# A planner learns that weight buffers take turns, and rounds the next weights after a block's first step

## The chip, the core and the metric

The kernel runs on one core of a Trainium2 chip. The metric is device time in microseconds: the median of three runs of the kernel before is 920.47 us (920.26 to 920.74). Engines are named as the profile names them: PE (TensorE, with PEld for its weight loads), DVE (VectorE), ACT (ScalarE), POOL (GpSimd), SP (SyncE).

## The reference

Two layers of a streaming encoder, with the same weights for a new stream of 512 frames (the prompt) and for 64 frames of a running one (the sample, with a cache of 1024 frames). Cut to what matters:

```python
def layer(x, ...):
    h = rms_norm(x, norm_g)
    u_p, z_p, q, k, v, qi, ki, wi, z_a, g_p, g_a = split(h @ w_in)
    pooled = causal means of u_p over 2, 4, 8, 16 frames, minus u_p, mixed by w_pool_mix
    br_pool = (pooled * silu(z_p)) @ w_pool_out
    q, k, qi, ki = rope(...)                       # 8 heads of 64; indexer 8 heads of 32
    score = sum_h wi * relu(qi . ki)               # the indexer; chunk-causal mask
    o = softmax(q . k over the top 128 (prompt) or 256 (sample) by score) @ v
    br_attn = (o * silu(z_a)) @ w_attn_out
    x = x + (sigmoid(g_p) * br_pool + sigmoid(g_a) * br_attn) @ w_o
    return x, k, v, ki, pool_state
y = rms_norm(x after two layers, final_norm_g)
```

All of it is float32, and so are the outputs.

## The kernel before

**Tiling.** The model's 1024 columns lie on the 128 partitions in 8 parts; the 576 frames (512 + 64) are the free dimension. All weights are cut into pieces of 128 x 1024, 57 in each layer. A piece comes from memory into a buffer `raw` (a load that SP issues). It is then split (`split_to`, L342): ACT rounds it to the matmul's format (the high part, `CAST whl<-raw`), ACT writes the raw weights' negative beside it (`ACTIVATE whl<-raw`), and POOL issues a DMA that adds the raw weights to it, which leaves the low part. Three buffers `whl` take turns. Activations are kept as a high part `h` and a low part `lo` as well.

**Blocks.** A block (`block`, L461) multiplies one piece by all frames: 8 steps (`step`, L440) of 6 matmuls of 128x288, which are high times high, high times low and low times high for each half of the frames. So a block is 48 matmuls, in the profile `mm<-quart,whl`. Into them other work is woven: the pooling mixer, the indexer's scores and the selection, the attention of the prompt by heads and query tiles (512, 384, 256 and 128 wide), then that of the sample.

**What sets the order.** The program is unrolled ahead of time. `Plan` (L62) runs its own clock for each engine while the program is written: `run` (L143) sets each instruction's start by when its operands and its engine are ready, by costs given for each kind of instruction. The woven work is written as generators. Each yields a condition (`need`, L208), and after each step of a block `pump` (L230) takes those whose condition holds by these clocks. `slot` (L176) is how most buffers tell the plan when a new tile of a ring can be written: not before the last use of the tile that it replaces. The `whl` buffers were not told of: the plan takes a new one as writable at once. On the chip each engine works its own instructions off in the order written, and a wait at the head of an engine's queue holds all that is behind it.

**The places in question.** At the start of a block its weights are taken and the piece three ahead is split (`block`, L461 to L463): ACT's two instructions and POOL's DMA are written ahead of the block's first matmul. At the start of layer 0, `Entry.first` (L498) rounds the eight parts of x on ACT as they arrive, and after the first of them `ki_split` rounds the indexer's key weights. Every instruction is written through one helper, so all rows of the profile bear line 262 (263 in the changed kernel).

Names: `sm` are score and transpose results, `mm` those of blocks (both in PSUM); `prob` and `quart` also hold probabilities, `tmp` anything of 128x576; `Ct` and `St` are the rope tables times the norm's factors, made by POOL; `qz`, `qzl` are the prompt's queries, `qzs` the sample's; `ident` marks a transpose; `stat` holds row sums.

Of the kernel before, what the change touches and what calls it, by code (L numbers as in the profile page):

```python
# [11 lines left out]
F32R = mybir.dt.float32r  # L12
# [3 lines left out]
P = 128  # L16
# [30 lines left out]
UNITS = 3  # L47
FIRST_H = ()
LAG = (1, 2)
DMA_US = 3.0  # L50
WARM = 11
NORM_A = 0
# [12 lines left out]
class Plan:  # L65
# [77 lines left out]
    def run(self, eng, op, args, kw):  # L143
# [18 lines left out]
        if eng == "dma" or op == "dma_start":  # L162
            n = 1
            for k in outs[0].shape[1:]:
                n *= k
            late = DMA_US + 4 * outs[0].shape[0] * n / 180e3
        for x in outs:
# [100 lines left out]
def encoder_step(ctx: ExitStack, tc: tile.TileContext, a: dict):  # L268
    nc = tc.nc
    plan = Plan()  # L270
# [5 lines left out]
    rot = ctx.enter_context(tc.tile_pool(name="rot", bufs=1))  # L276
# [7 lines left out]
    def tmp(n=T, dtype=F32):  # L284
        return rot.tile([P, 608], dtype, name="tmp", tag="tmp", bufs=NTMP)[:, :n]
# [16 lines left out]
    def ps_mm():  # L302
        return plan.slot("mm", 2, psum.tile([P, 2, 512], F32, name="mm", tag="mm", bufs=2), False)

    def ps_s(hold=False):
        return plan.slot("sm", 4, psum.tile([P, 512], F32, name="sm", tag="sm", bufs=4), hold)
# [22 lines left out]
    for l in range(DEPTH):  # L329
        pieces += [(l, j) for j in range(a["n_pieces"])]  # L330
    raw_of, split_of = {}, {}
    state = {"load": 0, "split": 0, "next": 0}

    def load_to(n):
        while state["load"] < min(n, len(pieces)):
            i = state["load"]
            l, j = pieces[i]
            raw_of[i] = raws()
            dma.dma_start(raw_of[i], a["w"][l, j])
            state["load"] += 1  # L340

    def split_to(n):  # L342
        while state["split"] < min(n, len(pieces)):
            i = state["split"]
            load_to(i + 1)
            x = raw_of.pop(i)
            w = rot.tile([P, 2, 1024], F32R, name="whl", tag="whl", bufs=3)
            act.copy(w[:, 0], x)

            act.activation(w[:, 1], x, AF.Copy, scale=-1.0)  # L350
            pool.dma_start(w[:, 1].bitcast(F32), x, accum_op=OP.add)
            plan.let(x)
            split_of[i] = w
            state["split"] += 1

    def split_first(i=0):

        load_to(i + 1)
        x = raw_of.pop(i)
        w = rot.tile([P, 2, 1024], F32R, name="whl", tag="whl", bufs=3)  # L360
        for c, eng in ((slice(0, 512), dve), (slice(512, 1024), pool)):
            act.copy(w[:, 0, c], x[:, c])
            eng.tensor_tensor(w[:, 1, c], x[:, c], w[:, 0, c].bitcast(F32), op=OP.subtract)
        plan.let(x)
        split_of[i] = w
        state["split"] = i + 1

    def weights():
        i = state["next"]
        state["next"] += 1  # L370
        split_to(i + 1)
        load_to(i + 4)
        w = split_of.pop(i)
        return w, i
# [60 lines left out]
    ps = ps_s()  # L435
# [3 lines left out]
    def step(ps, w, xh, xl, k, nk, off=0, parts=((0, 0, HT), (1, HT, T)), low=(False, True)):  # L439

        c = slice(off + k * P, off + (k + 1) * P)
        wh, wl = w[:, 0, c], w[:, 1, c]
        for s, t0, t1 in parts:
            cols = slice((k % 2) * T + t0, (k % 2) * T + t1)
            h, lo = xh[k // 2][:, cols], xl[k // 2][:, cols]
            o = ps[:, s, :t1 - t0]
            if False in low:  # L450
                pe.matmul(o, lhsT=wh, rhs=h, start=k == 0, stop=False)
                pe.matmul(o, lhsT=wh, rhs=lo, start=False, stop=False)
            if True in low:
                pe.matmul(o, lhsT=wl, rhs=h, start=False, stop=k == nk - 1)

    def product(ps, w, xh, xl, nk, off=0):
        for k in range(nk):
            step(ps, w, xh, xl, k, nk, off)
            plan.pump()

    def block(xh, xl, nk=8):  # L461
        w, i = weights()
        split_to(i + 3)  # L463
        ps = ps_mm()
        product(ps, w, xh, xl, nk)
        return ps

    class Entry:
# [29 lines left out]
        def first(self, k, x, ki_split):  # L498

            c = slice((k % 2) * T, (k % 2 + 1) * T)  # L500
            g = gains[:, self.l, k:k + 1]
            h = self.h[k // 2][:, c]
            if k in FIRST_H:
                dve.tensor_scalar(h, x, g, None, op0=OP.mult)
            else:
                act.activation(h, x, AF.Copy, scale=g)
            if k == 0:
                ki_split()
            dve.scalar_tensor_tensor(self.lo[k // 2][:, c], x, g, h.bitcast(F32), op0=OP.mult, op1=OP.subtract)
            self.rest.append(x)  # L510
            if k == 7:
                for i, x in enumerate(self.rest):
                    sq = tmp() if i else self.acc
                    act.activation(sq, x, AF.Square)
                    if i:
                        dve.tensor_tensor(self.acc, sq, self.acc, op=OP.add)
# [27 lines left out]
    def prepare_ki(l):  # L544
        rk = prob()
        rki = rk[:, :320].rearrange("p (k c) -> p k c", k=8)
        dma.dma_start(rk[:, :320], a["w_ki"][l])

        def ki_split():
            act.copy(kiw[:, :, 0:40], rki)  # L550
            (pool if l else dve).tensor_tensor(kiw[:, :, 64:104], rki, kiw[:, :, 0:40].bitcast(F32), op=OP.subtract)

        return ki_split

    def layer(l, x, arrive):
# [12 lines left out]
        if l:  # L568
            split_to(n + 3)
# [8 lines left out]
        ps_k, ps_q0 = [ps_s(True) for _ in range(2)], ps_mm()  # L578
        lag = (0, 0) if l else LAG
        for k in range(8 + lag[1]):  # L580
            if k == 7:
                plan.finish(*x.coming)
            if 3 <= k + 2 < 8:
                arrive(k + 2)
            if k < 8:
                c = (k % 2) * T
                for s in range(2):
                    cols = slice(c + s * HT, c + (s + 1) * HT)
                    pe.matmul(ps_k[s][:, :HT], lhsT=kiw[:, k], rhs=xh[k // 2][:, cols], start=k == 0, stop=False)
                for s in range(2):  # L590
                    cols = slice(c + s * HT, c + (s + 1) * HT)
                    pe.matmul(ps_k[s][:, :HT], lhsT=kiw[:, k], rhs=xl[k // 2][:, cols], start=False, stop=k == 7)
            if lag[0] <= k < 8 + lag[0]:
                step(ps_q0, w, xh, xl, k - lag[0], 8, low=(False,))
            if k >= lag[1]:
                step(ps_q0, w, xh, xl, k - lag[1], 8, low=(True,))
                plan.pump()
            if l == 0 and k == 4:
                split_first(1)
            if l == 0 and k == 6:  # L600
                split_to(3)
# [244 lines left out]

        def u_job(g):
            ps = block(xh, xl)
            ux = tmp(608)
            pool.memset(ux[:, 0:PST], 0.0)  # L850
# [39 lines left out]

        def z_job(g):
            ps = block(xh, xl)
            zt = tmp()
            dve.tensor_tensor(halves(zt), ps[:, :, :HT], halves(Rt), op=OP.mult)
# [35 lines left out]
        def sigmoid_gate():  # L930
            ps = block(xh, xl)
            zt = tmp()
            dve.tensor_tensor(halves(zt), ps[:, :, :HT], halves(Rt), op=OP.mult)

            def go():
                yield lambda: need("act", zt)
                act.activation(zt, zt, AF.Sigmoid)

            start(go(), 2)
            return zt  # L940
# [6 lines left out]
        def po_job(m2):  # L947
            if m2 == 0:
                plan.finish(*mixes)
            w, n = weights()  # L950
            split_to(n + 3)
            for i in range(2):
                ps = ps_mm()
                product(ps, w, ah, al, 4, off=512 * i)
                pb = sgs.pop(2 * m2 + i)
                dve.tensor_tensor(halves(pb), ps[:, :, :HT], halves(pb), op=OP.mult)

                def go(pb=pb, m=2 * m2 + i):
                    yield lambda: need("dma", pb)
                    dma.dma_start(mp_d[l][m], pb)  # L960

                start(go(), 2)
            if m2 == 3:
                let(*ah, *al)
# [492 lines left out]
    ki_split = prepare_ki(0)  # L1457
# [7 lines left out]
    def arrive(k):  # L1465
        x.first(k, xt[k // 2][:, (k % 2) * T:(k % 2 + 1) * T], ki_split)
        if k == 7:
            plan.let(*xt)
        if k == 1:
            split_first()  # L1470
# [110 lines left out]
```

## Time and profile before

| | us |
|---|---|
| median of 3 runs | 920.47 |
| profiled execution | 921.1 |
| its span, first to last instruction | 919.3 |
| PE busy | 894.8 (97%) |
| DVE busy | 668.3 (73%) |
| ACT busy | 593.2 (65%) |
| POOL busy | 202.1 (22%) |

The mean granted clock of PE is 0.995. By the chain of work that ended last, PE holds 68% of the span, DVE 14%, ACT 13%. A row of the timeline below gives the start, the time until the last of its instructions ended, the engine, the operation and its tiles, the count, and in brackets how long the engine had been idle before it and what released it. Times are microseconds from the start of the span. The rows stand in order of time, each engine works its rows in order, so what stands late in one engine's rows can be held by a row before it.

### The profile page before, as it was taken

The numbers are of one execution on the slowest core, as the hardware profiler recorded it, in microseconds if no ns is written. First come the engines' busy times: TensorE is split into PE (matmuls) and PEld (weight loads), VectorE is DVE, ScalarE is ACT, GpSimd is POOL, SyncE is SP. The second block draws the span as 40 slices with busy tenths as digits, with TensorE's granted clock in tenths as the row PEclk, the third lists the DMA queues.
The fourth block names the chain that finished last, engine by engine and source line by source line (L and its number), as shares of the span: only waits on it lengthen the run. The fifth ranks groups of instructions, "written<-read, shape, count | busy, mean of one in ns | idle before, by whom it ended". The sixth has DMA issues, their size and how long they took to land.

```text
span 919.3 us, 17403 instructions
## 1 busy us (share of the span) xinstructions
PE 894.8 (97%) x6613; PEld 881.4 (96%) x6613; DVE 668.3 (73%) x1554; ACT 593.2 (65%) x1056; POOL 202.1 (22%) x217
## 2 busy tenths in 40 slices
PE   8999999999999999999999999999999999999996
PEld 7999999999999999999999999999999999999995
DVE  6996899799896677362359779988989875755314
ACT  7556534588898975564537564446889988556642
POOL 3111211134432300112211121113443222011121
PEclk9999999999999999999999999999999999999998
DMA  7756587766555675779976667786655548648862
GB/s 266 187 140 164 134 214 189 173 161 160 125 145 147 179 199 150 186 202 240 263 191 175 154 151 163 191 203 180 165 139 133 157 124 221 189 135 222 236 146 104
DMA packets 54500, 160.97 MB, mean 175 GB/s; under 512 B 6736, under 2 KB 9040, under 8 KB 54416
## 3 DMA queue, kind: packets, MB, share of 16 engines
q0 software_dynamic: 16416, 59.78, 34.8%
q1 hardware_dynamic: 38000, 100.08, 32.2%
q8 instruction: 52, 0.85, 0.4%
q14 instruction: 32, 0.26, 0.1%
HBM read 85.37 MB, written 14.69 MB: 109 GB/s over the span
## 4 chain that ended last, share of the span: by engine, by line
PE 68%; DVE 14%; ACT 13%; issue 3%; DMA 1%; POOL 1%; SPq 0%; DVEq 0%; ACTq 0%; POOLq 0%
PE mm L262 57%; PE sm L262 11%; DVE tmp L262 6%; DVE quart L262 6%; ACT prob L262 4%; ACT whl L262 3%; ACT quart L262 2%; ACT qz L262 1%; ACT L262 1%; DVE big L262 1%; ACT tmp L262 1%; POOL tmp L262 1%; DMA raw<-in_w_dram 1%; DMA prob<-in_c_v_dram 1%; DVE prob L262 0%
## 5 line engine op out<-in xcount | busy, mean ns | idle before, releaser
L262 PE MATMUL mm<-quart,whl 128*128 128x288 f32 (+1 forms) x5568 | 780.4, 296 | 1.6 <-ACT quart L262 1.2
L262 PEld LDWEIGHTS mm<-quart,whl 128*128 128x128 f32 x5568 | 754.2, 188 | 4.3 <-ACT quart L262 2.0
L262 POOL DMA_DIRECT2D whl<-raw x114 | 99.3, 871 | 648.9 <-ACT whl L262 433.1
L262 ACT CAST whl<-raw 128x1024 fp32r<-128x1024 f32 (+1 forms) x118 | 121.8, 1034 | 133.2 <-PE mm L262 88.7
L262 ACT ACTIVATE whl<-raw 128x1024 fp32r<-128x1024 f32 x114 | 120.4, 1056 | 0.0
L262 ACT ACTIVATE prob<-prob,stat 128x128 f32<-128x128 f32 (+3 forms) x128 | 67.5, 554 | 6.8 <-DVE stat L262 6.4
L262 DVE SCALAR_TENSOR_TENSOR quart<-prob,wcol,quart 128x256 f32<-128x256 f32 (+4 forms) x60 | 42.1, 704 | 26.4 <-ACT prob L262 25.1
L262 ACT ACTIVATE prob<-sm 128x256 f32<-128x256 f32 (+4 forms) x72 | 33.5, 481 | 38.4 <-PE sm L262 38.4
L262 DVE MATCH_REPLACE8 quart<-stat,quart 128x256 f32<-128x256 f32 (+2 forms) x96 | 51.1, 539 | 0.0
L262 DVE MAX8 stat<-quart 128x8 f32<-128x256 f32 (+2 forms) x96 | 47.3, 541 | 0.0
L262 DVE MAX8 quart<-quart 128x8 f32<-128x544 f32 x64 | 46.3, 723 | 1.2
L262 DVE MATCH_REPLACE8 quart<-quart 128x544 f32<-128x544 f32 x64 | 45.4, 709 | 0.0
L262 DVE TENSOR_TENSOR tmp<-tmp 128x576 f32<-128x576 f32 (+7 forms) x62 | 44.3, 720 | 1.3
L262 DVE TENSOR_TENSOR quart<-quart 128x576 fp32r<-128x576 f32 (+6 forms) x30 | 26.4, 881 | 21.5 <-ACT quart L262 21.0
L262 DVE TENSOR_TENSOR big<-sm,big 128x512 fp32r<-128x512 f32 (+1 forms) x64 | 28.9, 483 | 16.3 <-ACT big L262 16.1
L262 ACT CAST quart<-tmp 64x512 fp32r<-64x512 f32 (+4 forms) x44 | 24.1, 566 | 22.0 <-POOL tmp L262 11.7
L262 ACT COPY prob<-sm 64x512 f32<-64x512 f32 (+1 forms) x24 | 12.3, 514 | 39.0 <-PE sm L262 38.6
L262 PE MATMUL sm<-quart,big 128*128 128x128 f32 (+3 forms) x176 | 32.2, 291 | 1.4 <-DVE tmp L262 1.4
L262 ACT CAST big<-sm 128x512 fp32r<-128x512 f32 (+2 forms) x72 | 28.0, 434 | 8.4 <-PE sm L262 8.0
L262 DVE SCALAR_TENSOR_TENSOR quart<-tmp,gains,quart 128x576 fp32r<-128x576 f32 x8 | 6.5, 818 | 31.6 <-ACT quart L262 31.6
L262 DVE CUSTOM_DVE_ANT_0 prob<-sm,quart 128x512 f32<-128x512 f32 (+2 forms) x48 | 25.8, 550 | 4.8 <-PE sm L262 4.8
L262 DVE TENSOR_TENSOR quart<-mm,tmp 128x576 f32<-128x576 f32 (+2 forms) x10 | 6.4, 638 | 29.3 <-PE mm L262 29.3
(157 smaller groups left out, 1025.5 us busy)
## 6 DMA issues: line engine op xcount, KB each, us to landing
raw<-in_w_dram SPq DMA_DIRECT2D x116, 512.0 KB, 4.9
whl<-raw POOLq DMA_DIRECT2D x114, 512.0 KB, 4.8
mp<-tmp SPq DMA_DIRECT2D x16, 288.0 KB, 3.3
tmp<-mp SPq DMA_DIRECT2D x16, 288.0 KB, 4.7
prob<-in_c_k_dram SPq DMA_DIRECT2D x16, 256.0 KB, 4.8
prob<-in_c_v_dram SPq DMA_DIRECT2D x16, 256.0 KB, 3.8
out_o_v_dram<-quart SPq DMA_DIRECT2D x8, 320.0 KB, 4.6
quart<-in_x_dram SPq DMA_DIRECT2D x8, 288.0 KB, 6.3
```

Of the source, the lines that this page charges most:

```text
L262: return f(*args, **kw)
```

## The change

Three edits. First, `whls(i)` makes the `whl` buffer, and from the fourth on tells the plan that it can be written from the last planned use of the buffer three pieces earlier. Second, the split of the piece three ahead is no longer written at the block's start, but in `product` after the block's first step (`SPLIT_AT = 0`) and after the `pump` behind that step. Third, in `Entry.first` the key weights are rounded ahead of the first part of x. The instructions are the same in kind and number (two calls of the plan's bookkeeping apart, which issue nothing); as the plan's clocks differ, the woven work falls elsewhere.

```diff
+SPLIT_AT = 0
...
+    def whls(i):
+        w = rot.tile([P, 2, 1024], F32R, name="whl", tag="whl", bufs=3)
+        whl_names.append(w.tensor.name)
+        if i > 2:
+            plan.wrote(w, plan.last[whl_names[i - 3]])
+        return w
+
     def split_to(n):
...
-            w = rot.tile([P, 2, 1024], F32R, name="whl", tag="whl", bufs=3)
+            w = whls(i)
             act.copy(w[:, 0], x)
...
-    def product(ps, w, xh, xl, nk, off=0):
+    def product(ps, w, xh, xl, nk, off=0, ahead=0):
         for k in range(nk):
             step(ps, w, xh, xl, k, nk, off)
             plan.pump()
+            if k == SPLIT_AT:
+                split_to(ahead)
 
     def block(xh, xl, nk=8):
         w, i = weights()
-        split_to(i + 3)
         ps = ps_mm()
-        product(ps, w, xh, xl, nk)
+        product(ps, w, xh, xl, nk, ahead=i + 3)
         return ps
...
             else:
+                if k == 0:
+                    ki_split()
                 act.activation(h, x, AF.Copy, scale=g)
-            if k == 0:
-                ki_split()
```

Three places show how the order moves. The first is POOL in layer 0, from the blocks of the pooling branch on: `DMA whl<-raw` is the delivery of a low part, the two products are the rope tables. Before:

```order
L262 DMA whl<-raw 128x1024
L262 MEMSET tmp 128x15
L262 DMA whl<-raw 128x1024 x5
L262 TENSOR_TENSOR Ct<-tmp,Rt 128x576
L262 TENSOR_TENSOR St<-tmp,Rt 128x576
L262 DMA whl<-raw 128x1024 x13
```

And now:

```order
L263 DMA whl<-raw 128x1024
L263 MEMSET tmp 128x15
L263 DMA whl<-raw 128x1024 x4
L263 TENSOR_TENSOR Ct<-tmp,Rt 128x576
L263 TENSOR_TENSOR St<-tmp,Rt 128x576
L263 DMA whl<-raw 128x1024 x14
```

The two products stand one delivery earlier; the second layer is alike.

The second is ACT at the sample's first softmax, which is the ACTIVATE over 1088 logits with `stat` for its sum. Before:

```order
L262 CAST big<-prob 128x8x64 x2
L262 CAST quart<-quart 128x2x512
L262 COPY prob<-quart 128x128
L262 CAST whl<-raw 128x1024
L262 ACTIVATE whl<-raw 128x1024
L262 ACTIVATE quart,stat<-quart,stat 128x1088
```

And now:

```order
L263 CAST big<-prob 128x8x64 x2
L263 CAST whl<-raw 128x1024
L263 ACTIVATE whl<-raw 128x1024
L263 CAST quart<-quart 128x2x512
L263 COPY prob<-quart 128x128
L263 ACT_TABLE_LOAD
L263 ACTIVATE quart,stat<-quart,stat 128x1088
L263 COPY big<-kss 128x2x64
L263 CAST big<-prob 128x512 x2
L263 CAST whl<-raw 128x1024
```

The softmax stood directly behind a split, and now stands ahead of the next one, behind a table load.

The third is PE at the end of the prompt's attention: `sm<-quart,qz` are scores, `sm<-ident,prob` the transposes of probabilities, `sm<-big,quart` the products with the values. Before:

```order
L262 MATMUL sm<-quart,qz 128x128
L262 MATMUL sm<-quart,qzl_85 128x128
L262 MATMUL mm<-quart,whl 128x288 x42
L262 MATMUL sm<-ident,prob 128x128
L262 MATMUL mm<-quart,whl 128x288 x12
L262 MATMUL sm<-big,quart 128x512 x2
```

And now:

```order
L263 MATMUL sm<-quart,qz 128x128
L263 MATMUL sm<-quart,qzl_85 128x128
L263 MATMUL mm<-quart,whl 128x288 x54
L263 MATMUL sm<-ident,prob 128x128 x3
L263 MATMUL mm<-quart,whl 128x288 x6
L263 MATMUL sm<-ident,prob 128x128 x2
L263 MATMUL mm<-quart,whl 128x288 x18
L263 MATMUL sm<-ident,prob 128x128
L263 MATMUL mm<-quart,whl 128x288 x30
L263 MATMUL sm<-big,quart 128x512 x2
```

Between the last 128-wide scores and the last transpose stood 42 products of a block; now 54 + 6 + 18 = 78. Counted in products from the first attention scores (the 1212th of the layer's blocks, in both), the last value products stood behind the 1926th and now stand behind the 1860th. The sample's first scores stood 30 products ahead of their transposes, and now stand 48 ahead.

In the w_o stage of layer 0 (its last eight blocks) the residual of each part of the model's columns gives ACT two instructions (`quart<-tmp,gains`, then `acc<-tmp` or `tmp<-tmp`). Before, two splits stood ahead of the first such pair, and then a split and a pair in turn; now one split stands ahead of it. So each split there now stands behind a pair that it stood ahead of.

## Rows read from the trace of the kernel before

**Rows 1.** The page's head: span, and busy time by engine.

```profile
span 919.3 us, 17403 instructions
PE 894.8 (97%) x6613; PEld 881.4 (96%) x6613; DVE 668.3 (73%) x1554; ACT 593.2 (65%) x1056; POOL 202.1 (22%) x217
```

**Rows 2.** Timeline of PE, its waits in layer 0.

```profile
98.97 0.50 PE L262 MATMUL sm<-quart,big 128*128 128x512 f32 x1 [0.70 <-DVE tmp L262]
...
219.50 0.77 PE L262 MATMUL sm<-ident,tmp 128*128 128x128 f32 x5 [0.91 <-ACT tmp L262]
...
250.43 0.55 PE L262 MATMUL sm<-ident,prob 128*128 128x128 f32 x3 [0.48 <-ACT quart L262]
...
321.09 0.33 PE L262 MATMUL sm<-ident,prob 128*128 128x128 f32 x1 [0.81 <-ACT prob L262]
...
335.78 0.63 PE L262 MATMUL sm<-ident,quart 128*128 128x128 f32 x4 [1.20 <-DVE quart L262]
```

**Rows 3.** Timeline of SP's queue, POOL and DVE, 77 to 100 us.

```profile
77.09 3.33 SPq L262 DMA_DIRECT2D tmp<-in_rope_dram  x2
...
85.30 0.86 POOL L262 DMA_DIRECT2D whl<-raw  x1 [6.33 <-PE sm L262]
...
93.94 1.75 POOL L262 TENSOR_TENSOR Ct<-tmp,Rt 128x576 f32<-128x576 f32 x1
95.34 1.73 POOL L262 TENSOR_TENSOR St<-tmp,Rt 128x576 f32<-128x576 f32 x1
...
94.07 3.56 DVE L262 SCALAR_TENSOR_TENSOR quart<-prob,wcol,quart 128x512 f32<-128x512 f32 x1 [1.80 <-ACT prob L262]
...
99.26 0.74 DVE L262 SCALAR_TENSOR_TENSOR quart<-prob,wcol,quart 128x512 f32<-128x512 f32 x1
```

**Rows 4.** Timeline of ACT and DVE, 317 to 336 us.

```profile
317.06 1.28 ACT L262 ACT_TABLE_LOAD   x1
...
318.75 1.03 ACT L262 CAST whl<-raw 128x1024 fp32r<-128x1024 f32 x1
...
331.43 1.05 ACT L262 CAST whl<-raw 128x1024 fp32r<-128x1024 f32 x1 [3.12 <-PE mm L262]
...
333.34 1.19 ACT L262 ACTIVATE quart<-quart,stat 128x1088 f32<-128x1088 f32 x1
...
334.85 0.79 DVE L262 TENSOR_SCALAR quart<-quart,stat 128x1088 f32<-128x1088 f32 x1
```

**Rows 5.** Stretch of the prompt's attention: us, PE, PEld, DVE, ACT, POOL, clock, DMA.

```profile
193.00:324.00 131.00, 128.12 (x945) 124.94 (x943) 106.09 (x278) 116.67 (x243) 44.52 (x42) 1.00 0.57 147
```

**Rows 6.** Layer 0's w_o: chain, POOL, landing, ACT, DVE, a stretch (as rows 5).

```profile
375.28 83.60 PE mm L262 x624
...
416.22 0.86 POOL L262 DMA_DIRECT2D whl<-raw  x1 [1.46 <-ACT whl L262]
DMA to landing us min/median/max: 10.4/10.4/10.4
...
415.72 0.76 ACT L262 ACTIVATE quart<-tmp,gains 128x576 fp32r<-128x576 f32 x1
416.38 0.67 ACT L262 ACTIVATE acc<-tmp 128x576 f32<-128x576 f32 x1
...
413.76 0.76 DVE L262 TENSOR_TENSOR tmp<-mm,tmp 128x576 f32<-128x576 f32 x1 [2.90 <-PE mm L262]
...
420.00:425.00 5.00, 5.00 (x39) 5.00 (x39) 0.76 (x1) 1.01 (x2) 0.00 (x0) 1.00 1.04 297
```

**Rows 7.** Timeline of ACT at the start.

```profile
8.21 1.14 ACT L262 CAST whl<-raw 128x512 fp32r<-128x512 f32 x2 [1.25 <-DMA raw<-in_w_dram]
```

**Rows 8.** The tail: POOL's last low part, its landing, DVE's read-out.

```profile
890.11 0.86 POOL L262 DMA_DIRECT2D whl<-raw  x1 [5.52 <-ACT whl L262]
DMA to landing us min/median/max: 4.5/4.5/4.5
...
897.61 0.49 DVE L262 TENSOR_TENSOR quart<-mm,tmp 128x320 f32<-128x320 f32 x1 [1.12 <-PE mm L262]
```

More of the change, by code (lines that the diff above doesn't have):

```diff
@@ L331, in encoder_step @@
     raw_of, split_of = {}, {}
+    whl_names = []
     state = {"load": 0, "split": 0, "next": 0}
@@ L359, in split_first @@
         x = raw_of.pop(i)
-        w = rot.tile([P, 2, 1024], F32R, name="whl", tag="whl", bufs=3)
+        w = whls(i)
         for c, eng in ((slice(0, 512), dve), (slice(512, 1024), pool)):
```

## The prediction

> **What bounds the kernel now.** I read the table of busy shares first: TensorE works 894.8 of 919.3 us and nothing else passes 73% [rows 1]; its granted clock is 1.00 in the stretches read below [rows 5, 6]. The change adds and removes no instruction of TensorE, so it can only take from the 24.5 us (919.3 − 894.8) in which TensorE stands, or add to them. Then I went to the timeline of TensorE alone, where a bracket behind a row says how long it stood and for whom. The reader is to see two things [rows 2]: the waits are short (0.5 to 1.2 us; the second layer repeats each of them, so one row stands for two), and each is for a row that another engine delivers a little late, none for weights. Third, the chain of waits, which gives the speed of undisturbed products: 624 from 375.28 on in 83.60 us, 0.134 us each, so 6.43 us for a block of 48 [rows 6]. With that, positions in TensorE's order become times.
>
> The program is an order fixed ahead by the plan; the engines work it off in turn. What the change does is therefore read as: which row now stands ahead of which, and is the wait behind it gone. The profiled execution took 921.1 us (span 919.3 and 1.8 around it), 0.63 above the median of 920.47; I sum against 921.1 and take 0.63 off.
>
> **A, the two rope products on GpSimd (−1.40).** At 93.94 and 95.34 GpSimd computes Ct and St, and VectorE's scalar_tensor_tensor, started between them at 94.07, takes 3.56 us where the same form takes 0.74 at 99.26 [rows 3]. It ends when St does (97.63 against 97.07), 2.8 us late. The mixer's read-out behind it is then late, and TensorE waits 0.70 at 98.97, and as long in the second layer [rows 2]. In the new order the pair stands one delivery of a low part earlier (four deliveries ahead, not five). The delivery that it then follows starts at 85.30; with its rounding about 1 us later and 0.86 to issue, the pair comes at about 87, with its tables asked for at 77.09 [rows 3]. VectorE has 1.80 us idle before 94.07 to make good what it loses there [rows 3]. I take the whole, 2 × 0.70 = 1.40. Bounds: −1.40, and 0 if the same slip only falls on another row (2.8 − 1.8 leaves 1.0, enough for a wait of 0.7); I take the first, as there is no wait of TensorE near 87 to lengthen.
>
> By the Trainium skill ("SBUF — State Buffer", "SBUF: two separate sides") VectorE and GpSimd share a port pair that the one that starts first holds for its whole instruction. By that rule VectorE would get its turn between Ct and St, slip by no more than one instruction (1.75), and the 1.80 idle would always absorb it: A would be −1.40 for sure. The row differs: VectorE stood through both (3.56), so the measured slip of 2.8 is what I bound by.
>
> **B, the sample's first softmax (−2.40).** ScalarE works in order. At 331.43 it stands 3.12 us for a weight buffer that TensorE still reads, and the exp over 1088 logits, ready and queued behind, starts only at 333.34; VectorE normalises at 334.85, and TensorE's transposes at 335.78 wait 1.20 [rows 4, 2]. The plan did not know of this buffer; now it does, and exp stands ahead of the next rounding. Against it, a table load (1.28, as at 317.06) now stands directly ahead of exp [rows 4]. For it, the transposes now stand 48 products behind the scores, not 30: 18 × 0.134 = 2.4 us more. Gained are 2.4 and the 3.12 that ScalarE stood, needed are 1.28 and the 1.20 of the wait: the wait goes, 2 × 1.20. Bounds −2.40 and 0.
>
> **C, the last 128-wide probabilities (−1.62).** A rounding of 1.03 and its negative copy stand at 318.75 between the exp and the scaling of this softmax, and TensorE waits 0.81 at 321.09 [rows 4, 2]. New: 78 products between these scores and their last transpose, not 42, 36 × 0.134 = 4.8 us more. The wait goes in both layers. Bounds −1.62 and 0.
>
> **D, the front of the prompt's attention (+1.0).** From the first attention scores to the eighth value product TensorE now has 648 block products between, not 714: 66 fewer, 8.8 us, in each layer. ScalarE is busy 116.67 of the 131.00 us of this stretch and VectorE 106.09 [rows 5]. Less the 1.4 roundings that fall out (66/48 × 2.1 = 2.9), ScalarE has 113.8 to do in 122.2 us, 93%. It fits, yet with less slack at each place: waits of 0.91 and 0.48 stand there now [rows 2], and the first nine transposes come 12 products (1.6 us) earlier, while the softmax that feeds them does not move. Nothing in the trace prices a packed front; bounds are −2.8 (2 × 1.39, both waits gone) and +17.6 (all of the 8.8 is waited back). I take +0.5 a layer, some 0.3 at the first transposes and 0.2 elsewhere, near the waits that are there today.
>
> **E, the weights in layer 0's w_o stage (+0.7).** Here the rounding now stands behind the residual's two ScalarE steps (0.76 and 0.67), which wait for VectorE's add (0.76): up to 2.2 us later [rows 6]. Normally that is covered by blocks of 6.43 us. But the DMA engines are full here (share 1.04), and a low part issued at 416.22 lands 10.4 us later, at 426.6 [rows 6]; the block that reads it is the fifth from the end of the chain's 624 products: 375.28 + 83.60 − 5 × 6.43 = 426.7. Three of the stage's deliveries are as tight, and this one stands for them; the others start late because the raw weights come late, which the change leaves alone. Bounds 0 (the DMA is only shifted within the same full stretch) and 3 × 1.43 = 4.3, the two ScalarE steps paid in full each time. I take 0.7, near the lower end: a shifted start finds the same queue emptier.
>
> **No cost.** At the start the key weights' rounding goes ahead of that of x: ScalarE then stands 1.25 for weights before 8.21 anyway. Two roundings of 512 take 1.14 there, so this one of 320 takes under 0.57, and that is its price if the cover were gone [rows 7]. At the end the last low part, issued 890.11 and landing 4.5 later, comes up to 2.2 later, 896.8; the block before it ends near 897.5, as VectorE's read-out at 897.61 shows [rows 8]. The loads of raw weights on SP follow the roundings later by a step, and have three to four blocks of lead.
>
> Sum: −1.40 − 2.40 − 1.62 + 1.0 + 0.7 = −3.72. 921.1 − 3.72 = 917.38, less 0.63: **916.7**.
>
> **The rivals.** Under about 0.2% (1.84 us: 918.6 to 922.3) a measurement of this kernel cannot be told from no change.
> R1, slower: the packed front makes TensorE wait. ScalarE at 93% in a chain of scores, softmax, transposes and values leaves no room for its own order, and half of the 8.8 us comes back as waits: +8.8 in place of +1.0, −1.40 − 2.40 − 1.62 + 8.8 + 0.7 = +4.08, 924.5. It decides from 6.6 us of new waits there (37% of 17.6). For it: the stretch already holds two of the five waits. Against it: the waits there are for single rows, and VectorE has 25 us free.
> R2, no change: weights come late in the w_o stage at the full bound, E = 4.3: −0.12, 920.3. For it: the landing of 10.4 and no spare at 426.7. Against: only three of its blocks are so tight.
> R3, no change: the change does not do what it says; the waits of A, B and C only move to the next row, and 1.0 is left of them: 919.5. For it: in an order worked off in turn a wait removed often meets the next, and ScalarE still rounds as much. Against: the orders show 18 and 36 products more at just these places.
>
> **How the numbers follow.** The forecast gets 0.57, with its own range of 914.0 (D at −1.0 and E at 0) to 919.2 (0.7 of A and 1.8 of B and C left). R1 0.17, R2 0.13, R3 0.13. So faster 0.57, within 0.2% 0.26, slower 0.17. The range reaches down to 913.5, where some of D's waits go too, and up to 921.5, past R2 and R3; most of R1 (0.15) and a little below (0.04) stay out.
>
> **What would show it.** A: Ct at about 87, no scalar_tensor_tensor of 3.5 us with a wait of TensorE behind it. B and C: no wait of TensorE at the sample's first transposes, nor at the last one of a 128-wide tile. D: the waits between the first scores and the eighth value product sum to 1.4 to 2.4 a layer; 5 or more is R1. E: short waits for weights at the starts of blocks after 415. I would be wrong above all if TensorE waits for ScalarE's probabilities all along the front, or if the long VectorE row turns up again with its wait.

## The result and the profile after

The changed kernel takes 910.17 us (909.75 to 910.41, 4 runs), the kernel before in the same comparison 920.61; the ratio is 0.9884, with a 95% interval of 0.9867 to 0.9902. It is faster, by 10.4 us, where 3.8 was forecast, and it lies below the range's lower end of 913.5.

The page's head of the changed kernel, to be held against [rows 1]:

```profile
span 908.0 us, 17405 instructions
PE 891.8 (98%) x6613; PEld 881.2 (97%) x6613; DVE 668.5 (74%) x1554; ACT 593.2 (65%) x1056; POOL 199.9 (22%) x217
```

Count and kind of the work are the same. TensorE's idle time falls from 24.5 to 16.2 us, 8.3 less. That is not the 11.3 by which the span shrinks: TensorE's "busy" falls by 3.0 as well, with the same 6613 instructions. The ends of matmuls are modelled, and part of a stall between two starts is told as busy. So a bracket understates a stall: the wait of 1.20 at 335.78 [rows 2] is 1.36 between the starts, beyond the 0.133 that the block product ahead of it takes undisturbed, and the one of 0.81 is 0.97.

Where the time went I read by the starts of the same block product in both traces (the 193rd, the 1201st and so on, which stand for the same place in the program):

| stretch | forecast | measured |
|---|---|---|
| start, to the fifth block | 0 | −0.61 |
| mixer and indexer, both layers (A) | −1.40 | −0.26 |
| attention, both layers (B, C, D) | −3.02 | −10.38 (5.17 and 5.21) |
| layer 0's w_o stage (E) | +0.7 | −0.36 |
| tail | 0 | +0.30 |
| sum | −3.72 | −11.31 |

The two profiled executions lie 11.35 apart (921.1 and 909.75). The stretch that matters is the attention. One row for each kernel shows it: the stretch's length, then the busy time of PE, PEld, DVE, ACT and POOL, the clock, and the DMA engines' share. Before:

```profile
193.00:375.00 182.00, 177.77 (x1322) 173.93 (x1321) 141.81 (x365) 146.95 (x298) 48.82 (x47) 1.00 0.59 154
```

And after:

```profile
192.00:370.00 178.00, 177.86 (x1331) 174.96 (x1330) 143.26 (x371) 148.25 (x302) 47.68 (x47) 1.00 0.61 157
```

TensorE stood 4.23 us there, and now stands 0.14. ScalarE does as much work as before, in less time (147 of 182 us, now 148 of 178), and TensorE hardly waits for it any more.

B and C came as forecast. In the changed kernel ScalarE loads its table at 319.08, exp follows, and the split stands behind it; TensorE's transposes carry no bracket, and neither does the last transpose of the 128-wide probabilities (C, at 305.75):

```profile
305.75 0.27 PE L263 MATMUL sm<-ident,prob 128*128 128x128 f32 x1
...
319.08 1.28 ACT L263 ACT_TABLE_LOAD   x1
320.38 1.21 ACT L263 ACTIVATE quart<-quart,stat 128x1088 f32<-128x1088 f32 x1
...
322.81 1.05 ACT L263 CAST whl<-raw 128x1024 fp32r<-128x1024 f32 x1
...
324.03 0.60 PE L263 MATMUL sm<-ident,quart 128*128 128x128 f32 x4
```

A did not. The pair of products moved as said, and took its victim along, rows that answer to [rows 3]:

```profile
86.27 1.77 POOL L263 TENSOR_TENSOR Ct<-tmp,Rt 128x576 f32<-128x576 f32 x1
87.66 1.75 POOL L263 TENSOR_TENSOR St<-tmp,Rt 128x576 f32<-128x576 f32 x1
...
86.29 3.55 DVE L263 SCALAR_TENSOR_TENSOR quart<-prob,wcol,quart 128x384 f32<-128x384 f32 x1 [1.71 <-ACT prob L263]
...
91.19 0.50 PE L263 MATMUL sm<-quart,big 128*128 128x512 f32 x1 [0.60 <-DVE tmp L263]
```

VectorE's row starts 0.02 us after Ct, stands until St is done (89.41), and TensorE waits 0.60 one delivery earlier instead of 0.70. St begins (87.66) before Ct's row ends (88.04), so the trace shows no moment between the two. By the Trainium skill ("SBUF — State Buffer", "SBUF: two separate sides") the one of the two engines that starts first holds the shared port pair for its whole instruction. Read strictly, VectorE would have had its turn when Ct ended; this is the second row that shows it did not.

The rows that I had left unread are GpSimd's in the attention's front. Before:

```profile
204.79 0.88 POOL L262 DMA_DIRECT2D whl<-raw  x1 [7.99 <-ACT whl L262]
205.36 1.77 POOL L262 TENSOR_TENSOR tmp<-tmp,St 128x576 f32<-128x576 f32 x1
207.20 1.44 POOL L262 TENSOR_TENSOR tmp<-tmp 128x576 f32<-128x576 f32 x1
208.59 1.30 POOL L262 TENSOR_TENSOR quart<-quart 128x512 fp32r<-128x512 f32 x1
```

And after:

```profile
201.35 1.29 POOL L263 TENSOR_TENSOR quart<-quart 128x512 fp32r<-128x512 f32 x1 [5.35 <-ACT quart L263]
202.72 0.46 POOL L263 TENSOR_TENSOR vss<-quart,vss 64x128 fp32r<-64x128 f32 x1
203.26 1.44 POOL L263 TENSOR_TENSOR tmp<-tmp,St 128x576 f32<-128x576 f32 x1
204.78 1.42 POOL L263 TENSOR_TENSOR tmp<-tmp 128x576 f32<-128x576 f32 x1
206.14 0.89 POOL L263 DMA_DIRECT2D whl<-raw  x1
```

A split has three instructions, and the third, the delivery of the low part, stands in GpSimd's queue. Before, it stood at that queue's head for 7.99 us until ScalarE had rounded, and the key's rope products and the values' low part waited behind it. Now the products run ahead of it, 2.4 us earlier (204.78 against 207.20 for the second rope product; 0.74 of it the changed kernel is ahead already when the attention begins), and the delivery finds its rounding done.

### The profile page after: what moved, and what is told of

It reads as the page before. It is cut to its first block, busy times and chain, and to the rows that moved or that the text cites. A ratio compares the mean times of both kernels' runs of the same rounds, so it can differ in the third digit from the quotient of the medians.

```text
span 908.0 us, 17405 instructions
## 1 busy us (share of the span) xinstructions
PE 891.8 (98%) x6613; PEld 881.2 (97%) x6613; DVE 668.5 (74%) x1554; ACT 593.2 (65%) x1056; POOL 199.9 (22%) x217
## 4 chain that ended last, share of the span: by engine, by line
PE 87%; DVE 6%; ACT 4%; POOL 1%; issue 1%; DMA 1%; SPq 0%; DVEq 0%; POOLq 0%; ACTq 0%
PE mm L263 73%; PE sm L263 14%; DVE tmp L263 3%; DVE quart L263 3%; ACT prob L263 1%; ACT quart L263 1%; POOL tmp L263 1%; DMA quart<-in_x_dram 1%; ACT whl L263 1%; ACT qz L263 0%; ACT L263 0%; SPq L263 0%; DVE rcol L263 0%; ACT tmp L263 0%; DVE acc L263 0%
## 5 line engine op out<-in xcount | busy, mean ns | idle before, releaser
L263 ACT ACTIVATE prob<-prob,stat 128x256 f32<-128x256 f32 (+3 forms) x128 | 67.7, 555 | 4.7 <-DVE stat L263 4.2
L263 DVE TENSOR_TENSOR tmp<-tmp 128x576 f32<-128x576 f32 (+7 forms) x62 | 42.4, 688 | 1.3
L263 DVE TENSOR_TENSOR tmp<-mm,tmp 128x576 f32<-128x576 f32 x28 | 21.0, 750 | 29.2 <-PE mm L263 29.0
L263 ACT ACTIVATE tmp<-quart 128x576 f32<-128x576 f32 (+2 forms) x24 | 14.4, 638 | 22.3 <-DVE quart L263 22.3
```

The source lines that it names most:

```text
L263: return f(*args, **kw)
```

## The experiments

**The edits one by one.** Each starts from the kernel before.

> The kernel before with the third edit alone (key weights rounded ahead of x); TensorE's order is that of before. If the 0.6 us that the changed kernel is ahead from its fourth block on come from this edit: 919.9, first key matmul near 6.0 instead of 6.87. If the start is bound by the weights, as I had predicted: 920.5, no change.

> The first edit alone: the plan knows that the weight buffers take turns, the split stays at the block's start. Theory P (the plan's knowledge is what packs the attention): 912 or less. Theories W and Q (the place of the split does it): within 1.5 us of before, 919 to 921, since 36 of TensorE's rows differ from before, against 262 in the changed kernel.

> The second edit alone: the split behind the block's first step, the plan not told of the buffers. TensorE's order is that of the changed kernel. Theories W and Q: all but the start's 0.6 of the gain, 910.8. Theory P: 917 or more, since ScalarE's order differs from the changed kernel's at the places where the plan should know of the buffer.

```diff
# first: ki_split() ahead of x0 alone
# second: whls(i) alone, and the split where it was
     def block(xh, xl, nk=8):
         w, i = weights()
+        split_to(i + 3)
# third: SPLIT_AT alone, with whls(i) not telling the plan
-            plan.wrote(w, plan.last[whl_names[i - 3]])
```

Measured against before: 1.0001 (0.9990 to 1.0011), 0.9988 (0.9979 to 0.9997) and 0.9883 (0.9868 to 0.9898), in us 920.81, 919.54 and 910.49. So the key weights' edit is too small to be seen in the time, though its profile is 0.5 to 0.8 ahead from the first product to the last. The plan's knowledge is worth about 1 us: it takes away the 1.20 at the sample's first transposes by itself and leaves the 0.8 of C, and a later wait in the sample's attention grows (0.63 at 353.18, where before had 0.15 at 353.20). The place of the split is the change: alone it gives the same order on TensorE, row for row, and the same time. My reason for B (the plan now knows of the buffer) was thus one of two; the split's new place does it without that knowledge.

**Place, or the order that the plan makes of it?** In these two the plan's clocks are run for one place of the split, and the split is written at the other.

> The split of each block is written behind its first step, but the plan's clocks are run as if it still stood at the block's start: every row of TensorE and VectorE stands as in before, only ScalarE's and GpSimd's rows of the split come later. Theory Q (a rounding at the head of ScalarE's queue holds back softmax work that is ready): most of the gain comes already with this, 915 or less. Theory W (what counts is the woven order that the plan makes with the split at its new place): 919 to 921.

> The mirror of the run before: the plan's clocks are run as in the changed kernel (split behind the first step), so every row of TensorE, VectorE and SP stands as there, but the split's rows are written at the block's start, ahead of the first step's woven work. If the woven order on TensorE is what the gain is made of: 909.5 to 912. If it is that ScalarE does the step's softmax work ahead of the 2.1 us of a split (and the plan knows of it): 915 or more, with TensorE's waits back behind ScalarE's prob and quart rows between the first attention scores and the eighth value product.

```diff
     def block(xh, xl, nk=8):
         w, i = weights()
+        s = split_plan(i + 3)          # takes the buffers, issues nothing
+        plan_split(*s)                 # clocks only (the other: real_split, rows only)
...
             if k == SPLIT_AT:
-                split_to(ahead)
+                real_split(*ahead)     # the other: plan_split
```

Both lose: 945.39 us, 1.0261 (1.0245 to 1.0276), and 925.06, 1.0043 (1.0026 to 1.0060). The first falls outside of both theories, far above either: putting the rows later is a loss where the plan does not reckon with it. In layer 0 it loses 6.3 us ahead of the attention and 5.1 in it. Rows of ACT and PE show one place:

```profile
97.69 0.68 ACT L263 ACTIVATE tmp<-tmp 128x576 f32<-128x576 f32 x1 [1.67 <-DVE tmp L263]
98.28 1.03 ACT L384 CAST whl<-raw 128x1024 fp32r<-128x1024 f32 x1
...
100.80 0.77 PE L263 MATMUL sm<-quart,big 128*128 128x512 f32 x1 [2.02 <-ACT prob L263]
```

ScalarE idles 1.67 us where the split stood before, then does the split ahead of the score rows (`prob`) that TensorE needs next, and TensorE stands 2.02. The second says that the order on TensorE, which is that of the changed kernel, is not enough for the gain. Its rows of POOL, ACT and PE at the attention's front show where it is lost:

```profile
205.30 0.88 POOL L386 DMA_DIRECT2D whl<-raw  x1 [8.04 <-ACT whl L385]
...
208.12 1.44 POOL L263 TENSOR_TENSOR tmp<-tmp,St 128x576 f32<-128x576 f32 x1
209.63 1.41 POOL L263 TENSOR_TENSOR tmp<-tmp 128x576 f32<-128x576 f32 x1
...
211.07 1.25 ACT L263 CAST quart<-tmp 64x512 fp32r<-64x512 f32 x2 [3.46 <-POOL tmp L263]
...
212.96 0.33 PE L263 MATMUL sm<-ident,prob 128*128 128x128 f32 x1 [2.48 <-ACT prob L263]
```

With the split early, the delivery is at GpSimd's head again for 8.04 us; the rope products run 5 us later than in the changed kernel, ScalarE stands 3.46 for them, its probabilities are queued behind, and TensorE stands 2.48.

**Which of the split's two queues?** GpSimd's delivery alone is moved behind the first step; ScalarE's two rows stay at the block's start. Once with the weave of before, where no other engine's row changes, and once with the weave of the changed kernel, which differs from the 925 us kernel in GpSimd's queue alone.

> The kernel before, in every row of PE, ACT, DVE and SP; only GpSimd's delivery of a low part is written behind the block's first step, as in the changed kernel, so the rope and value products that this step brings stand ahead of it and no longer wait for ScalarE's split. If GpSimd's queue is what holds before back at 205 us: products there start 2 to 4 us earlier, and 916 to 919.5. If only ScalarE's order counts: 920 to 922.

> The changed kernel's weave with ScalarE's two rows of the split at the block's start, but GpSimd's delivery behind the first step as in the changed kernel; it differs from the 925 us kernel in GpSimd's queue alone. If GpSimd's queue makes those 15 us: 910 to 914. If ScalarE's order makes them: 922 to 926.

```diff
+            real_round(*s)             # at the block's start: ScalarE's two rows
...
             if k == SPLIT_AT:
-                split_to(ahead)
+                real_low(*ahead)       # behind the first step: GpSimd's delivery
```

918.66 us, 0.9959 (0.9944 to 0.9973), and 914.42, 0.9919 (0.9903 to 0.9935). In the second, POOL and ACT at the same place:

```profile
202.52 1.41 POOL L263 TENSOR_TENSOR tmp<-tmp,St 128x576 f32<-128x576 f32 x1
204.01 1.43 POOL L263 TENSOR_TENSOR tmp<-tmp 128x576 f32<-128x576 f32 x1
205.39 0.88 POOL L388 DMA_DIRECT2D whl<-raw  x1
...
205.51 1.25 ACT L263 CAST quart<-tmp 64x512 fp32r<-64x512 f32 x2
```

ScalarE no longer waits for GpSimd. By the ratios, as the runs were measured at different times, the 925 us kernel and the changed one lie 14.6 us apart; 11.4 of these come back with GpSimd's row alone, and the other 3.2 go with ScalarE's two rows. The second fell a little outside of both expectations (910 to 914, 922 to 926), far nearer to GpSimd's; the first is as GpSimd's theory had it. With the old weave, too, GpSimd's row alone is worth 1.6 us in each layer's attention.

What ScalarE's rows are worth shows in the stalls. Counted are, in both layers' attention, all places where TensorE's next start comes over 0.26 us later than the running matmul's columns take undisturbed (0.133 us for 288, others in proportion), and of these the ones where a row of a split had ended on ScalarE in the 2.6 us ahead of the restart:

| kernel | stalls, us | behind a split, us |
|---|---|---|
| before | 11.3 | 7.9 |
| delivery alone late, old weave | 8.4 | 7.1 |
| delivery alone late, new weave | 6.7 | 6.7 |
| the changed kernel | 0.3 | 0 |

The delivery's place removes most of the stalls that no split stands ahead of (3.4 us before, 1.3 with the old weave, none with the new), and those that stand behind one go only when ScalarE's two rows move as well. That a split ended shortly ahead of a stall does not by itself show that it made it; that these stalls go with the rows' place does. The whole gain came only with both moved and the plan reckoning with them.

**The rope tables.**

> The changed kernel with the two rope table products on VectorE in place of GpSimd; TensorE's and ScalarE's order is that of the changed kernel. If the two engines' clash is the cause of the 3.55 us row: no VectorE row over 1 us there, 2 x 0.75 more work against 2.8 less, TensorE's waits of 0.60 and 0.6 at the mixer's second half gone: 909.0 to 909.6. If that wait has another cause (ScalarE or VectorE late by itself): 910.2, no change.

```diff
-                yield lambda: need("pool", raw)
-                pool.tensor_tensor(t, raw, Rt, op=OP.mult)
+                yield lambda: need("dve", raw, room=0.0)
+                dve.tensor_tensor(t, raw, Rt, op=OP.mult)
```

908.92 us, 0.9863 (0.9847 to 0.9880). VectorE's rows:

```profile
88.01 0.62 DVE L263 SCALAR_TENSOR_TENSOR quart<-prob,wcol,quart 128x384 f32<-128x384 f32 x1 [1.73 <-ACT prob L263]
...
93.94 0.75 DVE L263 TENSOR_TENSOR Ct<-tmp,Rt 128x576 f32<-128x576 f32 x1
94.61 0.75 DVE L263 TENSOR_TENSOR St<-tmp,Rt 128x576 f32<-128x576 f32 x1
```

No row of VectorE over 1 us, no wait of TensorE there, and this stage is 0.98 and 1.03 us ahead of before in the two layers, where the changed kernel is 0.13 ahead. So the clash is the cause of A's waits; taking GpSimd out of it removes them, moving the pair does not. This version beats both kernels; against the changed one by 1.2 us, which the two intervals, overlapping, leave open.

**Is the first step the right place?**

> The changed kernel with the split behind the block's second step instead of its first. If the rule is general (softmax work that is ready at a block's start should go ahead of the split): 909 to 912. If the changed kernel's weave is a lucky one: 913 to 921, with long waits in the attention again. Weights come 0.8 us later than in the changed kernel, which costs up to 0.8 in each block of layer 0's w_o stage that is tight, 2.4 in all.

> The same behind the third step. General rule: 909 to 913, as the woven work is again ahead, and up to 1.6 us more lateness of the weights in tight blocks. Lucky weave: 913 to 921.

```diff
-SPLIT_AT = 0
+SPLIT_AT = 1          # the other: 2
```

917.97, 0.9962 (0.9952 to 0.9973), and 918.69, 0.9963 (0.9951 to 0.9975). Faster than before, but about 8 us behind the changed kernel. Both fall where the expectations put a lucky weave, and stalls are back in the attention; what neither expectation named is that TensorE there also waits for weights (1.0 and 2.2 us for the low parts' landing, against none). So these two do not tell luck from the price of later weights.

**The weave by itself.** The plan's settings are moved a little, at the new place of the split and at the old one; every one of them makes another order.

> The changed kernel with the plan's MARGIN (how long data for TensorE must have been ready by the plan's clocks) at 0.35 instead of 0.40 us: another weave, a quarter as far from the changed one (116 of TensorE's rows) as that is from before. If the place behind the first step is good by itself: 909 to 912. If the weave of the changed kernel is a lucky one: 913 to 921.

> The same with MARGIN at 0.45 (224 of TensorE's rows). Place good by itself: 909 to 912. Lucky weave: 913 to 921.

> The kernel before with MARGIN at 0.35 (206 rows of TensorE differ). If the split at the block's start is what costs: 919 to 923, like before. If before was an unlucky weave: 911 to 917.

> The same with MARGIN at 0.45 (164 rows). Split at the block's start costs: 919 to 923. Unlucky weave: 911 to 917.

> The changed kernel with the plan's EPS_T (how far ahead of an engine's clock its data may be) at 0.10 instead of 0.15 us; 228 of TensorE's rows differ. If the place behind the first step is better by itself, by 2 to 3 us a layer on average: 911 to 917. If only single weaves are lucky: 917 to 923.

> The changed kernel with ROOM (how far ScalarE's and VectorE's clocks may run ahead of TensorE's when new scores are taken) at 0.9 instead of 1.0 us; 338 rows. Place better by itself: 911 to 917. Single weaves: 917 to 923.

> The kernel before with EPS_T at 0.10; 356 rows of TensorE differ. Place better by itself: 918 to 923, as for the old place so far. Single weaves, whatever the place: the same spread as for the new place, some as low as 911 to 917.

> The kernel before with ROOM at 0.9; 318 rows. Place better by itself: 918 to 923. Single weaves: as low as 911 to 917 as likely as for the new place.

```diff
-MARGIN = 0.4
+MARGIN = 0.35         # or 0.45; or EPS_T = 0.10 for 0.15; or ROOM = 0.9 for 1.0
```

| setting | new place, us (ratio) | old place, us (ratio) |
|---|---|---|
| as it is | 910.17 (0.9884) | 920.61 |
| MARGIN 0.35 | 913.80 (0.9925) | 921.91 (1.0007) |
| MARGIN 0.45 | 923.10 (1.0019) | 917.95 (0.9970) |
| EPS_T 0.10 | 909.21 (0.9865) | 914.54 (0.9931) |
| ROOM 0.9 | 914.45 (0.9922) | 916.33 (0.9943) |
| mean | 914.1 | 918.3 |

The 95% intervals reach 0.1 to 0.3% to each side. Three of the eight fell outside of both of their ranges (923.10 and 909.21 at the new place, 917.95 at the old), so neither theory as I put it holds. The place is worth 4 us on the mean, but single plans spread by 5.5 (new) and 3.0 (old) around theirs, so that five of each leave the 4 with an uncertainty of 2.8: I do not call it shown. What is shown is that the changed kernel's 10.4 is at the good end of what its place gives, and that the worst plan at the new place is slower than before. That one has stalls of 9.7 us in the attention, counted as above, none of them behind a split: what the place is meant to remove is gone in it too, and the weave lost nearly as much elsewhere. By the starts the two layers' attention takes 374.5 us there, 373.6 before and 363.2 in the changed kernel. One row of it:

```profile
288.25 0.33 PE L263 MATMUL sm<-ident,prob 128*128 128x128 f32 x1 [1.29 <-ACT prob L263]
```

## Why the prediction was wrong

**D failed, in sign and size**, and nothing else would have carried the time out of the range. It said that the packed front costs 1.0, with −2.8 as the best case. B and C measure −4.66 by the starts (2 × 1.36 and 2 × 0.97), so −5.7 is left; some 0.6 of it is a small wait in the sample's attention (353.20, twice) that no term named, and about −5.1 is D's. Two steps of it went wrong. First, I took the packing by itself as a price: the softmax that feeds the transposes would not move while the transposes come sooner. It did move, since the products on GpSimd that stand ahead of it no longer wait for a split: with the delivery alone late and every other engine's rows as before, the wait of 0.91 at 219.50 [rows 2] is gone (the row below carries no bracket). I named GpSimd's queue for A and for E and never read it for the attention, though the split's third instruction stands there and the row of 7.99 us idle was to be had. Second, the best case counted the two larger waits of the front by their brackets, 1.39 a layer; by the starts five stalls stood there that sum to 3.0, each about 0.16 longer than its bracket, with that part told as busy.

```profile
220.95 0.77 PE L263 MATMUL sm<-ident,tmp 128*128 128x128 f32 x5
```

**A was wrong in its mechanism's last step.** That 1.80 us of idle VectorE would take up the slip was true of the row that had the idle ahead of it, and the idle is there because that row waits for ScalarE. The pair started just ahead of another row of the same kind. −0.26 for −1.40; the other bound, 0, was the right one.

**B and C were right**, each gone in both layers, and worth an eighth to a fifth more than their brackets. The reason given for B held for the first edit alone (919.54), but the time came with the second.

**E charged a price that did not come**; its lower bound, 0, was the right one. There is no wait for weights after 415: TensorE's row there is unbroken, as it was before, and the low part issued at 412.30 lands after 8.2 us, not 10.4:

```profile
411.79 40.83 PE L263 MATMUL mm<-quart,whl 128*128 128x288 f32 x305
```

It measures −0.36 for +0.7; where the 0.36 come from stays open.

**The start and the tail**, taken at nothing, gave −0.6 and +0.3. The first is within what the start differs between executions with the same rows: the third block begins at 28.32 in the changed kernel's profile and at 30.04 in that of the one with its tables on VectorE.

**The rivals.** R1 had the mechanism turned round: ScalarE's share in the front did rise, from 89% to 92%, and no wait came of it. R2 and R3 did not happen. No rival had the front gaining, and the range had no room for the time: even with D at its best case of −2.8 and E at 0 the sum gives 912.25.

## What to carry to other kernels

Where a piece of work has instructions on several in-order queues, moving it moves all of them: look at each queue for what stood behind it and was ready, here 2 to 5 us of products behind a DMA issue that waited for another engine. An order made by a planner's clocks is best issued as it was planned: with the split's rows moved by one step (0.8 us) against the plan, the kernel before lost 24 us and the changed one about 15, though the delivery alone, moved so, gained 3.8. And one plan of a planner whose order shifts with every setting says little about the rule behind it: small changes of a setting moved this kernel by 14 us.

## What was not expected of the hardware

A VectorE row that starts with GpSimd's first of two rows stands through both of them: 3.56 and 3.55 us for rows that take 0.74 and 0.61 undisturbed. And the sum of TensorE's busy time is not a constant of the program: 894.8 and 891.8 us for the same 6613 matmuls, at granted clocks of 0.995 and 0.996.
